# mLSTM heads: the gates' exponent rows reach 128 partitions by a transfer from memory instead of by a selection product

## The chip, the core and the metric

The kernel runs on one core of one Trainium2 chip. The metric is the device time of one execution in microseconds (us), median of several runs; less is better. A core has TensorE (PE; its weight loads are shown apart as PEld), VectorE (DVE), ScalarE (ACT), GpSimd (POOL) and SyncE (SP). Each takes its instructions in the order in which they were queued; they meet at semaphores. Transfers between memory (HBM) and the core's SBUF are issued from a queue of SP, ACT or POOL and run on 16 DMA engines. Products land in PSUM, which has eight banks of 128 x 512 f32.

## The reference

A two-layer encoder over 512 tokens of width 1024. Layer A mixes with a four-head mLSTM (head width 192) and a memory attention, layer B with a band attention and a memory attention; both are followed by a gated MLP with a causal convolution. Only the mLSTM of layer A is touched. Its core, as the reference writes it for chunks of tokens:

```python
b = jnp.cumsum(lf, axis=-1)
d = b[..., :, None] - b[..., None, :] + ii[..., None, :]
d = jnp.where(tril, d, -jnp.inf)
m_inter = b + m_st[..., None]
m_t = jnp.maximum(m_inter, jnp.max(d, axis=-1))
s = jnp.einsum('bhtd,bhsd->bhts', qq, kk) * jnp.exp(d - m_t[..., None])
num = jnp.einsum('bhts,bhse->bhte', s, vv) + ...
```

The exponent of the weight between key s and query t of a head is a sum of a term of the key and a term of the query. With the keys on the partitions, the key's term is a column (one number per partition) and the query's term is a row along the free dimension that is the same on all 128 partitions.

## The kernel before, in words

Everything is kept transposed: channels or keys on the partitions, the 512 tokens (S) along the free dimension, in four blocks (TT) of 128 (P). f32 products are made of three products of a high and a low part (`mm3`, lines L175 to L177 of the profile), so each weight tile is loaded by SP (`wr`, three buffers), cast to its high part by ACT (`wh`, L136) and subtracted to its low part by DVE (`wl`, L137).

The order of the work is woven. A generator does a stage and yields; `weave(job, filler, each)` advances a filler generator by `each` steps per yield of the job, so that TensorE has projections to do while a head's chain runs over ACT, DVE and POOL. Below that a scheduler orders each engine's queue when the program is built: an instruction that is ready may be put ahead of others, except those passed to `pin`, which stay behind everything written before them on their engine. Tiles come from pools by tag with a fixed number of buffers: 57 `u`, 8 `t`, 2 `pt`, 2 `bias` in SBUF and 3 `mm`, 3 `sc`, 2 `tr` banks in PSUM (`pmm`, `psc`, `ptr` in the profile).

The part that matters here:

- At the start two tiles `sel` (L115 memset, L118 casts) are made, with ones in the row that belongs to a head, and `maskf`, `ident` and others.
- `gate_rows` (L1026) turns the gates into rows. It is woven into the second half of the value projection and the first query and key tiles at 0.3 step per yield. Scans on DVE (L1055, L1062) give the running sums `br` and maxima `mr` of four heads on four partitions. Then, for each key block s, the query term from token 128 s on is written to `rr` (L1074, L1083). L1085 and L1086 finish the floor of the denominator. L1091 and L1092 split each row into a high part and a low part 32 partitions further down, in two zeroed `u` tiles `rp` (L1050). Eight tiny transposes (from L1096 on) make columns of `ar` and `mr`: `acol` (L1098), the key term, and the floor (L1099, an Exp on ACT).
- `mlstm_head` (L1144) runs once per head. `weighted_scores(s)` handles key block s with the n = 512 - 128 s queries from there on. It takes an `sc` bank, spreads head h's row over all partitions with one product (L1155, `sel` times `rp`, which also adds the high and the low part), and ACT takes Exp of it with the bias `acol` into a `t` tile (L1157). POOL zeroes the upper triangle of the diagonal block (L1159). After a yield come the scores in a second `sc` bank (three products and two, L175 to L177 and L525), DVE multiplies scores and weights (L1168), and ACT and DVE split the result into `pt` (L136, L137). `products(s)` multiplies these with the values into two `tr` banks. The order is scores 0, 1, 2, products 0, scores 3, products 1, 2, 3; then squares (L1195), the norm (L1202 to L1209, L237, L250) and the gate (L1216).
- Beside the heads the fillers run: `qk_tile` (accumulator L1108 in a `t` tile, taps L1111, Silu L1112), `o_tile` (L1126), query projections for the memory attention, whose zero halves POOL sets (L505), memory attention (Exp L582), then parts of the output projection.
- Later, POOL also issues the transfers of layer B's bias: a row of the table to 128 rows in memory (L1258), a corner (L1260), and from there to a `bias` tile (L1327). The final norm's gain comes by two transfers of one row of 512 to 128 partitions (L1409), also into `bias` tiles.

Of the kernel before, what the change touches and what calls it, by code (L numbers as in the profile page):

```python
# [9 lines left out]
F32 = mybir.dt.float32  # L10
F32R = mybir.dt.float32r
I32 = mybir.dt.int32
AF = mybir.ActivationFunctionType
ALU = mybir.AluOpType
AX = mybir.AxisListType

P = 128
D = 1024
S = 512
KT = D // P  # L20
TT = S // P
MEM = 256
AW = 768
AH = 4
# [26 lines left out]
def f(ap):  # L51
    return ap.bitcast(F32)
# [3 lines left out]
def trunk(  # L56
# [18 lines left out]
    nc = tc.nc  # L75
    V, A, G = nc.vector, nc.scalar, nc.gpsimd

    cpool = ctx.enter_context(tc.tile_pool(name="cpool", bufs=1))
    pool = ctx.enter_context(tc.tile_pool(name="pool", bufs=1))
    psum = ctx.enter_context(tc.tile_pool(name="psum", bufs=1, space=bass.MemoryType.PSUM))  # L80

    bufs = {"wr": 3, "wh": 3, "wl": 3, "u": 57, "t": 8, "pt": 2, "s": 16, "rb": 3, "bias": 2}
    pbufs = {"mm": 3, "sc": 3, "tr": 2}
    count = [0]
    dram = ctx.enter_context(tc.tile_pool(name="dram", bufs=1, space=bass.MemoryType.DRAM))

    def sb(tag, shape, dtype=F32):
        count[0] += 1
        return pool.tile(shape, dtype, tag=tag, name=f"{tag}{count[0]}", bufs=bufs[tag])

    def ps(tag):
        count[0] += 1
        return psum.tile([P, S], F32, tag=tag, name=f"p{tag}{count[0]}", bufs=pbufs[tag])

    def small(n=4):
# [3 lines left out]
    ident = cpool.tile([P, P], F32, name="ident")  # L99
# [9 lines left out]
        out=maskf, in_=maskf, pattern=[[1, P]], base=0, channel_multiplier=-1,  # L109
        compare_op=ALU.is_ge, fill=NEG,  # L110
    )

    sels = [cpool.tile([P, AH, P], F32R, name=f"sel{i}") for i in range(2)]
    for i, sel in enumerate(sels):
        G.memset(f(sel), 0.0)  # L115
        for s in (2 * i, 2 * i + 1):
            q = slice(32 * s, 32 * s + AH)
            V.tensor_copy(sel[q], ident[q, 32 * s : 32 * s + AH].unsqueeze(2).to_broadcast([AH, AH, P]))  # L118
    eps = cpool.tile([P, 1], F32, name="eps")
    V.memset(eps, EPS)  # L120

# [11 lines left out]
    pin = tc.keep_in_program_order  # L133
# [32 lines left out]
    def weights(*args):  # L166
        return parts(load(*args))
# [5 lines left out]
    def mm3(o, lh, ll, rh, rl, first, last, more=False):  # L173

        nc.tensor.matmul(o, lh, rh, start=first, stop=False, skip_group_check=more)  # L175
        nc.tensor.matmul(o, lh, rl, start=False, stop=False, skip_group_check=more)  # L176
        nc.tensor.matmul(o, ll, rh, start=False, stop=last, skip_group_check=more)  # L177
# [250 lines left out]
    with tc.manual_schedule(engines={mybir.EngineType.PE, mybir.EngineType.Activation, mybir.EngineType.DVE}):  # L428
# [9 lines left out]
        for q in range(KT // 2 + 1):  # L438
            if q < KT // 2:
# [6 lines left out]
                hi, lo = sb("u", [P, S], F32R), sb("u", [P, S], F32R)  # L446
# [571 lines left out]
    e, u, c, r = (cpool.tile([P, TT, AH], F32, name=f"gate{i}") for i in range(4))  # L1018
    tot = cpool.tile([AH, 16], F32, name="tot")
    acol = cpool.tile([P, TT, AH], F32, name="acol")  # L1020
    floor2 = cpool.tile([P, TT, AH], F32, name="floor2")
    RO = [0, 512, 896, 1152, 1280]

    rp = []

    def gate_rows():  # L1026

        V.tensor_copy(ic, gt[:, :, :AH])
        V.scalar_tensor_tensor(e, fg, -1.0, fg, op0=ALU.mult, op1=ALU.min)
        A.activation(e, e, AF.Exp)  # L1030
        V.tensor_scalar(u, e, 1.0, None, op0=ALU.add)
        A.activation(lf, u, AF.Ln)
        V.scalar_tensor_tensor(c, u, -1.0, e, op0=ALU.add, op1=ALU.subtract)
        V.reciprocal(r, u)
        yield
        pin(V.tensor_mul(c, c, r))
        V.tensor_tensor(out=lf, in0=lf, in1=c, op=ALU.subtract)
        V.scalar_tensor_tensor(lf, fg, 0.0, lf, op0=ALU.min, op1=ALU.subtract)
        yield
        yield  # L1040
        lfp, icp = ps("tr"), ps("tr")
        for T in range(TT):
            nc.tensor.transpose(lfp[:AH, T * P : (T + 1) * P], lf[:, T, :], ident)
            nc.tensor.transpose(icp[:AH, T * P : (T + 1) * P], ic[:, T, :], ident)
        yield
        lfr, br, ar, mr = (sb("t", [P, S])[:AH, :] for _ in range(4))
        rr = [sb("t", [P, S]) for _ in range(2)]
        rp.extend(sb("u", [P, S], F32R) for _ in range(2))
        for t in rp:
            G.memset(f(t), 0.0)  # L1050
        pin(V.tensor_copy(lfr, lfp[:AH, :]))
        yield
        for T in range(TT):
            sl = slice(T * P, (T + 1) * P)
            pin(V.tensor_tensor_scan(br[:, sl], ones[:AH, :], lfr[:, sl], 0.0, ALU.mult, ALU.add))  # L1055
        yield
        pin(V.tensor_tensor(out=ar, in0=icp[:AH, :], in1=br, op=ALU.subtract))
        yield
        carry = 0.0
        for T in range(TT):  # L1060
            sl = slice(T * P, (T + 1) * P)
            pin(V.tensor_tensor_scan(mr[:, sl], ar[:, sl], ar[:, sl], carry, ALU.max, ALU.max))  # L1062
            if T < TT - 1:
                e_ = (T + 1) * P - 1
                V.tensor_tensor(out=tot[:, T : T + 1], in0=mr[:, e_ : e_ + 1], in1=br[:, e_ : e_ + 1], op=ALU.add)
                carry = tot[:, T : T + 1]
            yield
        for s in range(TT):
            off = None
            for T in range(s, TT):  # L1070
                sl = slice(T * P, (T + 1) * P)
                dst = rr[s // 2][64 * (s % 2) : 64 * (s % 2) + AH, sl]
                if T == s:
                    pin(V.tensor_scalar(dst, mr[:, sl], -1.0, None, op0=ALU.mult))  # L1074
                else:
                    end = br[:, T * P - 1 : T * P]
                    if off is None:
                        off = end
                    else:
                        k = 4 + 4 * s + T - s  # L1080
                        V.tensor_tensor(out=tot[:, k : k + 1], in0=off, in1=end, op=ALU.add)
                        off = tot[:, k : k + 1]
                    V.tensor_scalar(dst, mr[:, sl], -1.0, off, op0=ALU.mult, op1=ALU.add)  # L1083
            yield
        pin(V.tensor_tensor(out=mr, in0=mr, in1=br, op=ALU.add))  # L1085
        V.tensor_scalar(mr, mr, -40.0, None, op0=ALU.max)  # L1086
        yield
        for s in range(TT):
            q, t = 64 * (s % 2), rp[s // 2]
            src, hi = rr[s // 2][q : q + AH, s * P :], t[q : q + AH, s * P :]  # L1090
            pin(V.tensor_copy(hi, src))  # L1091
            V.tensor_tensor(out=t[q + 32 : q + 32 + AH, s * P :], in0=src, in1=f(hi), op=ALU.subtract)  # L1092
            yield
        tp = ps("tr")
        for T in range(TT):
            nc.tensor.transpose(tp[:, T * AH : (T + 1) * AH], ar[:, T * P : (T + 1) * P], ident[:AH, :AH])  # L1096
            nc.tensor.transpose(tp[:, 16 + T * AH : 16 + (T + 1) * AH], mr[:, T * P : (T + 1) * P], ident[:AH, :AH])
        pin(V.tensor_copy(acol, tp[:, :16].rearrange("p (t h) -> p t h", t=TT)))  # L1098
        A.activation(floor2, tp[:, 16:32].rearrange("p (t h) -> p t h", t=TT), AF.Exp, scale=-2.0)  # L1099
# [44 lines left out]
    def mlstm_head(h):  # L1144
# [4 lines left out]
        pt = sb("pt", [P, 5 * S], F32R)  # L1149

        def weighted_scores(s):
            n = S - s * P
            sl = slice(s * P, (s + 1) * P)
            r = ps("sc")
            nc.tensor.matmul(r[:, :n], sels[s % 2][:, h, :], rp[s // 2][:, s * P :], start=True, stop=True)  # L1155
            e = sb("t", [P, S])
            A.activation(e[:, :n], r[:, :n], AF.Exp, bias=acol[:, s, h : h + 1])  # L1157

            G.affine_select(  # L1159
                out=e[:, :P], in_=e[:, :P], pattern=[[1, P]], base=0, channel_multiplier=-1,  # L1160
                compare_op=ALU.is_ge, fill=0.0,
            )
            yield
            o = ps("sc")
            kf, qf = ks[full], qs[full]
            mm3(o[:, :n], kf[0][:, sl], kf[1][:, sl], qf[0][:, s * P :], qf[1][:, s * P :], True, False)
            head_scores(o[:, :n], odd, qs[sh], slice(s * P, S), ks[sh], sl, False, True)
            V.scalar_tensor_tensor(e[:, :n], o[:, :n], DH**-0.5, e[:, :n], op0=ALU.mult, op1=ALU.mult)  # L1168
            split(pt[:, RO[s] : RO[s + 1]], pt[:, 1280 + RO[s] : 1280 + RO[s + 1]], e[:, :n])
            yield  # L1170
# [3 lines left out]
        def products(s):  # L1174
            if not nums:
                nums.extend(ps("tr") for _ in range(2))
            for o, c in zip(nums, (3 * P, 2 * P) if odd else (0, P)):
                mm3(
                    o[:, s * P :], vh[hp][s][:, c : c + P], vl[hp][s][:, c : c + P],
                    pt[:, RO[s] : RO[s + 1]], pt[:, 1280 + RO[s] : 1280 + RO[s + 1]], s == 0, s == TT - 1,  # L1180
                )
# [88 lines left out]
    for j in range(KT):  # L1270
        wh, wl = weights(rows(ffn_w_down[0], j * P, P, FT - LAST, FT), LAST, P)
# [175 lines left out]
    n = LAST // 2  # L1447
    for hf in range(2):
# [6 lines left out]
        for Ts, pieces in groups:  # L1455
            for c in pieces:
                if c.start:
                    os_[Ts[0]] = ps("mm")
                for u in range(n):
# [3 lines left out]
                    wh, wl = ws[u]  # L1463
# [61 lines left out]
```

## Time and profile before

| | us |
|---|---|
| median of 3 runs | 1197.71 (1197.57 to 1198.04) |
| span of the profiled execution | 1197.4 |
| PE busy | 1186.5 |
| DVE busy | 967.3 |
| ACT busy | 718.4 |
| POOL busy | 123.3 |
| first and last selection product (L1155) | start at 105.3 and 238.0 |

How to read the rows that follow. A row of the order of time has start, duration, engine, line, operation, output tile, input tiles, shape, count, and in brackets how long the engine had been idle and what it waited for. A row of groups has the count behind the x, then busy time and mean ns of one, then idle time before them with what ended most of it. A row of waits says who waited for whom, the total in us, how often, and the longest. A row of one line has the durations of one in ns as min/median/max and the first and the last start. A row of transfers has the issuing queue, the count, the KB of each and the median us from issue to landing. Buffer numbers are left out of tile names.

### The profile page before, as it was taken

What the parts mean: (1) busy time and instruction counts of PE and PEld (TensorE: products, weight loads), DVE (VectorE), ACT (ScalarE), POOL (GpSimd) and SP (SyncE); (2) the same over time, 40 slices, a digit from 0 to 9 for tenths busy, and PEclk for the clock granted to TensorE, in tenths of its full rate; (3) what the DMA queues carried; (4) which work ended last, traced back from release to release, by engine and by line L of the source; (5) the groups of instructions that cost most, each with busy time, mean ns of one, the idle gap of its engine ahead of it and who ended that gap; (6) DMA issues with size and microseconds to landing.
All of it is one profiled execution on the core that took longest, in us unless ns stands there. A gap on an engine that the chain in (4) does not pass through costs nothing.

```text
span 1197.4 us, 18206 instructions
## 1 busy us (share of the span) xinstructions
PE 1186.5 (99%) x6735; PEld 1039.1 (87%) x6735; DVE 967.3 (81%) x1772; ACT 718.4 (60%) x1290; POOL 123.3 (10%) x206
## 2 busy tenths in 40 slices
PE   9999999999999999999999999999999999999997
PEld 8988888888889989999888888888889988999986
DVE  6778688878978888888698888997897888888855
ACT  5646577655655555555575667776565655555545
POOL 1200101000021111111021000001001011011100
PEclk9999999999999999999999999999999999999999
DMA  8634111454266666665563223146336466665551
GB/s 283 212 92 123 54 54 57 134 152 133 88 157 162 153 162 155 151 144 129 152 189 120 89 71 99 55 130 201 116 89 150 110 138 141 141 141 136 121 158 71
DMA packets 199131, 155.97 MB, mean 130 GB/s; under 512 B 7976, under 2 KB 179458, under 8 KB 199042
## 3 DMA queue, kind: packets, MB, share of 16 engines
q1 hardware_dynamic: 183906, 119.74, 34.2%
q0 software_dynamic: 14560, 34.02, 13.7%
q8 instruction: 53, 0.87, 0.3%
q10 hardware_dynamic: 576, 1.05, 0.2%
q14 instruction: 36, 0.29, 0.1%
HBM read 126.27 MB, written 32.44 MB: 133 GB/s over the span
## 4 chain that ended last, share of the span: by engine, by line
PE 93%; DMA 2%; ACT 2%; DVE 2%; issue 0%; SPq 0%; ACTq 0%; DVEq 0%
PE pmm L175 15%; PE pmm L176 15%; PE pmm L177 15%; PE ptr L175 6%; PE ptr L177 6%; PE ptr L176 6%; PE pmm L791 6%; PE psc L177 5%; PE psc L175 5%; PE psc L176 5%; PE pmm L790 3%; PE psc L525 2%; DMA wr<-in_mem_w_kv_dram 2%; PE ptr L1352 1%; PE ptr L1373 1%; PE ptr L1374 1%
## 5 line engine op out<-in xcount | busy, mean ns | idle before, releaser
L175 PE MATMUL pmm<-u,wh 128*128 128x512 f32 (+1 forms) x872 | 309.1, 355 | 0.3 <-ACT u L136 0.2
L176 PE MATMUL pmm<-u,wh 128*128 128x512 f32 (+1 forms) x872 | 306.3, 351 | 0.0
L177 PE MATMUL pmm<-u,wl 128*128 128x512 f32 (+1 forms) x872 | 306.3, 352 | 0.0
L137 DVE TENSOR_TENSOR wl<-wr,wh 128x1024 fp32r<-128x1024 f32 (+3 forms) x172 | 199.8, 1163 | 55.1 <-ACT wh L136 53.1
L136 ACT CAST wh<-wr 128x1024 fp32r<-128x1024 f32 (+3 forms) x172 | 172.1, 1002 | 99.8 <-PE pmm L176 45.2
L177 PEld LDWEIGHTS pmm<-u,wl 128*128 128x128 f32 x872 | 164.5, 189 | 20.9
L175 PEld LDWEIGHTS pmm<-u,wh 128*128 128x128 f32 x872 | 164.5, 189 | 18.7 <-ACT u L136 1.1
L176 PEld LDWEIGHTS pmm<-u,wh 128*128 128x128 f32 x872 | 164.7, 189 | 18.3 <-DVE u L137 0.5
L175 PE MATMUL ptr<-u,wh 128*128 128x512 f32 x272 | 106.7, 392 | 0.0
L177 PE MATMUL ptr<-u,wl 128*128 128x512 f32 x272 | 106.1, 390 | 0.0
L176 PE MATMUL ptr<-u,wh 128*128 128x512 f32 x272 | 105.9, 389 | 0.0
L759 POOL DMA_DIRECT2D xspill<-t x64 | 55.5, 867 | 462.5 <-ACT t L758 457.1
L136 ACT CAST u<-pt 128x512 fp32r<-128x512 f32 x102 | 62.8, 618 | 47.2 <-DVE pt L881 47.1
L137 DVE TENSOR_TENSOR u<-pt,u 128x512 fp32r<-128x512 f32 x102 | 69.9, 689 | 11.2 <-ACT u L136 8.5
L175 PE MATMUL psc<-u,wh 128*128 128x256 f32 (+1 forms) x232 | 76.1, 328 | 0.0
L177 PE MATMUL psc<-u,wl 128*128 128x256 f32 (+1 forms) x232 | 75.9, 327 | 0.0
L176 PE MATMUL psc<-u,wh 128*128 128x256 f32 (+1 forms) x232 | 75.9, 327 | 0.0
L791 PE MATMUL pmm<-u,u 128*128 128x512 f32 x192 | 69.6, 397 | 0.0
L943 ACT ACTIVATE t<-t 128x512 f32<-128x512 f32 x34 | 21.5, 632 | 79.4 <-DVE t L666 79.4
L827 DVE TENSOR_TENSOR t<-t,pmm 128x256 f32<-128x256 f32 x72 | 30.2, 420 | 45.0 <-ACT t L825 45.0
L758 ACT COPY t<-ptr 128x512 f32<-128x512 f32 x64 | 37.4, 584 | 42.8 <-PE ptr L177 42.8
L666 DVE SCALAR_TENSOR_TENSOR t<-t,cols,t 128x511 f32<-128x511 f32 x80 | 59.6, 746 | 3.7 <-ACT t L673 3.7
(305 smaller groups left out, 2671.5 us busy)
## 6 DMA issues: line engine op xcount, KB each, us to landing
wr<-in_ffn_w_up_dram SPq DMA_DIRECT2D x54, 512.0 KB, 4.5
wr<-in_ffn_w_down_dram SPq DMA_DIRECT2D x38, 512.0 KB, 4.1
pt<-in_ffn_w_up_dram SPq DMA_DIRECT2D x34, 512.0 KB, 6.0
xspill<-t POOLq DMA_DIRECT2D x64, 256.0 KB, 5.2
wr<-in_a_w_in_dram SPq DMA_DIRECT2D x20, 512.0 KB, 3.7
xspill<-u POOLq DMA_DIRECT2D x32, 256.0 KB, 2.7
u<-xspill SPq DMA_DIRECT2D x32, 256.0 KB, 5.1
wr<-in_w_kv_dram SPq DMA_DIRECT2D x12, 512.0 KB, 3.8
```

The source lines that it names most:

```text
L136: high = A.copy(hi, src) if on_act else V.tensor_copy(hi, src)
L137: low = V.tensor_tensor(out=lo, in0=src, in1=f(hi), op=ALU.subtract)
L175: nc.tensor.matmul(o, lh, rh, start=first, stop=False, skip_group_check=more)
L176: nc.tensor.matmul(o, lh, rl, start=False, stop=False, skip_group_check=more)
L177: nc.tensor.matmul(o, ll, rh, start=False, stop=last, skip_group_check=more)
L525: nc.tensor.matmul(o, a, b, start=first and i == 0, stop=i == 1)
L666: V.scalar_tensor_tensor(acc[:, n:], src[:, : S - n], self.fw[:, c * FT + j : c * FT + j + 1], acc[:, n:], op0=ALU.mult, op1=ALU.add,)
L758: A.copy(t, o)
L759: G.dma_start(xspill[j], t, accum_op=ALU.add)
L790: nc.tensor.matmul(r[:, :H], w[1][:, k], p[i - 1][:, :H], start=False, stop=False, skip_group_check=True)
L791: nc.tensor.matmul(r, w[0][:, k], p[i - 1], start=False, stop=k == n - 1, skip_group_check=True)
L827: V.tensor_tensor(out=o, in0=o, in1=r[:, H:], op=ALU.add)
```

## The change

The rows are not spread by TensorE any more. After the row of block s is in `rr`, POOL issues a write of it, in f32, to a tile `exponents` in memory. When the four writes are issued, POOL issues the first four spreads (head 0, blocks 0 to 3), each a transfer that reads one row 128 times into a `bias` tile. In `weighted_scores` Exp reads that tile, and right behind it POOL issues the spread of the step four further on, that is of the same block of the next head, ahead of the masking. The selection tiles, the split of the rows with its four yields, and the two zeroed `u` tiles go. The tag `bias` has four buffers instead of two, also for layer B and the final norm.

```diff
-    bufs = {"wr": 3, "wh": 3, "wl": 3, "u": 57, "t": 8, "pt": 2, "s": 16, "rb": 3, "bias": 2}
+    bufs = {"wr": 3, "wh": 3, "wl": 3, "u": 57, "t": 8, "pt": 2, "s": 16, "rb": 3, "bias": 4}
...
-    sels = [cpool.tile([P, AH, P], F32R, name=f"sel{i}") for i in range(2)]
-    for i, sel in enumerate(sels):
-        G.memset(f(sel), 0.0)
-        for s in (2 * i, 2 * i + 1):
-            q = slice(32 * s, 32 * s + AH)
-            V.tensor_copy(sel[q], ident[q, 32 * s : 32 * s + AH].unsqueeze(2).to_broadcast([AH, AH, P]))
...
+    NEXT = 4
     RO = [0, 512, 896, 1152, 1280]
 
-    rp = []
+    exponents = dram.tile([TT, AH, S], F32, name="exponents")
+    order = [(h, s) for h in range(AH) for s in range(TT)]
+    spreads = {}
+
+    def spread_exponents(i):
+        if i < len(order):
+            h, s = order[i]
+            row = exponents[s, h : h + 1, s * P :]
+            spreads[h, s] = sb("bias", [P, S])[:, : S - s * P]
+            src = bass.AP(tensor=row.tensor, offset=row.offset, ap=[[0, P], [1, S - s * P]])
+            pin(G.dma_start(spreads[h, s], src))
...
         rr = [sb("t", [P, S]) for _ in range(2)]
-        rp.extend(sb("u", [P, S], F32R) for _ in range(2))
-        for t in rp:
-            G.memset(f(t), 0.0)
...
                     V.tensor_scalar(dst, mr[:, sl], -1.0, off, op0=ALU.mult, op1=ALU.add)
+            q = 64 * (s % 2)
+            pin(G.dma_start(exponents[s, :, s * P :], rr[s // 2][q : q + AH, s * P :]))
             yield
+        for i in range(NEXT):
+            spread_exponents(i)
...
-        for s in range(TT):
-            q, t = 64 * (s % 2), rp[s // 2]
-            src, hi = rr[s // 2][q : q + AH, s * P :], t[q : q + AH, s * P :]
-            pin(V.tensor_copy(hi, src))
-            V.tensor_tensor(out=t[q + 32 : q + 32 + AH, s * P :], in0=src, in1=f(hi), op=ALU.subtract)
-            yield
...
-            r = ps("sc")
-            nc.tensor.matmul(r[:, :n], sels[s % 2][:, h, :], rp[s // 2][:, s * P :], start=True, stop=True)
             e = sb("t", [P, S])
-            A.activation(e[:, :n], r[:, :n], AF.Exp, bias=acol[:, s, h : h + 1])
-
+            A.activation(e[:, :n], spreads.pop((h, s)), AF.Exp, bias=acol[:, s, h : h + 1])
+            spread_exponents(order.index((h, s)) + NEXT)
```

## The prediction

> **What bounds the kernel now.** I read the page's head and engine shares first, then the stretch in which the mLSTM heads run as one window, then what TensorE waited for, then its order of time around the product that is removed.
>
> ```profile
> span 1197.4 us, 18206 instructions
> PE 1186.5 (99%) x6735; PEld 1039.1 (87%) x6735; DVE 967.3 (81%) x1772; ACT 718.4 (60%) x1290; POOL 123.3 (10%) x206
> 80.00:245.00 165.00, 164.80 (x838) 138.65 (x836) 129.32 (x256) 109.61 (x189) 10.74 (x22) 1.00 0.30 87
> PE psc L175 <- ACT t L1157: 0.2, 1, 0.2
> PE pmm L175 <- ACT u L136: 0.2, 1, 0.2
> ```
>
> The third line is the window from 80 to 245 us: busy time of PE, PEld, DVE, ACT and POOL, then granted clock, DMA share and GB/s. PE is busy for 164.80 of 165.00 us at full clock, DVE for 78% and ACT for 66%, and all PE waits from 100 to 300 us are the two lines of 0.2 us. So in this stretch a matmul that disappears should shorten the kernel by the slot it held, and a delay elsewhere costs only what is longer than PE's reserve of queued work. That slot is not its listed duration, because matmuls overlap: it is the distance to the next start.
>
> ```profile
> 105.26 0.40 PE L1155 MATMUL psc<-u,sel 128*128 128x512 f32 x1
> 105.50 0.39 PE L175 MATMUL pmm<-u,wh 128*128 128x512 f32 x1
> 105.73 0.40 PE L176 MATMUL pmm<-u,wh 128*128 128x512 f32 x1
> ...
> 108.00 0.34 PE L1155 MATMUL psc<-u,sel 128*128 128x384 f32 x1
> 108.18 0.40 PE L175 MATMUL pmm<-u,wh 128*128 128x512 f32 x1
> ...
> 111.17 0.28 PE L1155 MATMUL psc<-u,sel 128*128 128x256 f32 x1
> 111.29 0.40 PE L175 MATMUL pmm<-u,wh 128*128 128x512 f32 x1
> ...
> 116.00 0.22 PE L1155 MATMUL psc<-u,sel 128*128 128x128 f32 x1
> 116.06 0.45 PE L175 MATMUL pmm<-u,wh 128*128 128x512 f32 x1
> 116.35 0.40 PE L176 MATMUL pmm<-u,wh 128*128 128x512 f32 x1
> ```
>
> **Part 1, the products.** Per head the four selection products hold 0.24, 0.18, 0.12 and 0.06 us. The product behind the last one takes 0.29 us to the next start where its like takes 0.23 (105.50 to 105.73), so the short one costs 0.12. That is 0.66 us a head and 2.6 us for four. Lower bound: 0.23 us per 512 columns, so 1280 columns give 0.57 us a head, 2.3 us in all. Upper bound: the 5.0 us that the line is listed as busy; it counts time in which the next product runs too, so no more than 0.3 of the way to it belongs in the range. I take 2.6, since the starts measure it directly.
>
> Each product also held a score bank until Exp had read it, and here PE met that once:
>
> ```profile
> L1155 PE MATMUL psc<-u,sel 128*128 128x512 f32 (+3 forms) x16 | 5.0, 311 | 0.0
> 235.61 0.44 PE L175 MATMUL psc<-u,u 128*128 128x384 f32 x1 [0.18 <-ACT t L1157]
> ```
>
> With half the demand on the three score banks that 0.2 us should go too. Sum on PE: -2.8 us.
>
> **Part 2, VectorE, the start and the buffers.** The high and low parts of the rows (L1091, L1092) leave DVE, and so do the selection casts at the start.
>
> ```profile
> L1092 DVE TENSOR_TENSOR u<-t,u 4x512 fp32r<-4x512 f32 (+3 forms) x4 | 1.9, 483 | 0.1
> L1091 DVE CAST u<-t 4x512 fp32r<-4x512 f32 (+3 forms) x4 | 1.2, 312 | 0.1
> L118 DVE CAST sel<-ident x4: 417/420/704, 2.2 to 3.8; 4x512 fp32r<-4x512 f32 x4
> ```
>
> That is 3.1 us around 84 to 94 us and about 2 us (four times 0.42 to 0.70) before 4.2 us. DVE is not the bound in either place, and PE's start waits for the first transfers, so I count 0 for both (between 0 and -0.4 us, the size of the waits above). Two `u` buffers become free and `rr` can be released when its writes have landed, which can only loosen. The steps of the gate rows that follow move four steps earlier in a weave of 0.3 step per yield, about 13 yields. They issue eight tiny transposes, one DVE copy and one ACT Exp, all before PE needs them: 0. Four `bias` tiles instead of two let the band attention's transfers start earlier, and nothing in the profile waits for those: 0.
>
> **Part 3, the row's way to 128 partitions.** Added are 4 writes of at most 8 KB and 16 transfers of 256, 192, 128 and 64 KB per head, all issued on POOL. Nearest rows: `rep<-maskf` for the small writes to memory, and `bias<-in_final_g`, which copies one row to 128 partitions just as here.
>
> ```profile
> rep<-maskf POOLq DMA_DIRECT2D x12, 16.0 KB, 3.5
> bias<-in_final_g_dram POOLq DMA_DIRECT2D x2, 256.0 KB, 4.7
> L1409 POOL DMA_DIRECT2D bias<-in_final_g_dram x2: 683/716/748, 807.5 to 808.9; - x2
> 82.25 0.22 DVE L1074 TENSOR_SCALAR t<-t 4x128 f32<-4x128 f32 x1
> 109.38 0.72 POOL L1159 TENSOR_SCALAR_AFFINE_SELECT t<-t 128x128 f32<-128x128 f32 x2 [66.00 <-ACT t L1157]
> 108.57 1.15 ACT L1157 ACTIVATE t<-psc,acol 128x512 f32<-128x512 f32 x2
> 136.06 0.69 ACT L1157 ACTIVATE t<-psc,acol 128x512 f32<-128x512 f32 x1 [1.92 <-PE psc L1155]
> 190.23 0.69 ACT L1157 ACTIVATE t<-psc,acol 128x512 f32<-128x512 f32 x1
> 234.87 1.16 ACT L1157 ACTIVATE t<-psc,acol 128x512 f32<-128x512 f32 x2
> ```
>
> The last row is computed at 82.5 us (the instruction at 82.25 takes 0.22). Write issued by 83.2, landed by 86.7; four spreads issued behind it by 89.6, the last landed by about 94.3. The first Exp ran at 108.57, so 14 us cover this. POOL stands at the waits for the row writes meanwhile, but it had nothing to do for 66 us. Later, a spread is issued when the Exp four steps back has freed its buffer, and its own Exp comes one head later: 27, 54 and 45 us by the three distances above, against under 6 us of issue and landing. Cost: 0. It is 4.7 us once per head with no cover, 19 us at most.
>
> POOL does gain a queue: at 12 of the 16 steps the masking of the diagonal block (L1159) stands behind a transfer's issue of 0.7 us, and DVE's multiplication (L1168) and the casts to `pt` wait for it. The reserve there is the smallest I found:
>
> ```profile
> 111.66 1.16 DVE L137 TENSOR_TENSOR pt<-t,pt 128x512 fp32r<-128x512 f32 x2 [0.22 <-ACT pt L136]
> 113.96 0.39 PE L175 MATMUL ptr<-pt,u 128*128 128x512 f32 x1
> ```
>
> The parts are done at 112.82 and used at 113.96: 1.1 us. Against the 0.7 us stands that Exp no longer waits for a product (4.2 us over four times, next line) and can run any time before the scores exist, so that the masking may be through by then. I count 0, and 12 times 0.7, 8.6 us, were the reserve gone at every step.
>
> ```profile
> L1157 ACT ACTIVATE t<-psc,acol 128x512 f32<-128x512 f32 (+3 forms) x16 | 8.2, 525 | 4.3 <-PE psc L1155 4.2
> ```
>
> The Trainium skill speaks against this part: SBUF — State Buffer, section "SBUF: two separate sides", says that transfers issued from GpSimd cannot have their descriptors written while VectorE holds the port pair that the two share, and gives about 3.1 us for an issue that takes 0.62 us alone. The issues in this trace don't show it: 0.68 to 0.75 us above, and the twelve `bias` issues of the band attention stay at 0.55 to 0.75 with DVE busy for 164 of 190 us. But POOL work does stretch here:
>
> ```profile
> L1159 POOL TENSOR_SCALAR_AFFINE_SELECT t<-t x16: 287/299/1254, 109.4 to 238.7; 128x128 f32<-128x128 f32 x16
> L1327 POOL DMA_DIRECT2D bias<-rep x12: 546/548/748, 627.5 to 782.7; - x12
> 620.00:810.00 190.00, 189.35 (x971) 157.22 (x970) 164.47 (x401) 131.96 (x299) 18.34 (x32) 1.00 0.33 99
> ```
>
> A masking of 0.30 us has taken 1.25 at worst, so such a block is worth 1 us a time. That is a rival below.
>
> **The sum.** The profiled execution spans 1197.4 us, 0.3 under the median of 1197.71. 1197.4 - 2.6 - 0.2 = 1194.6, and with the 0.3 that lies around it **1194.9 us**.
>
> **The rivals.**
>
> (B) *Part is given back.* ACT takes its queue in order. Where an Exp is placed ahead of its transfer's landing, or between two Silus so that it brings a pair of table loads, what stands behind it is late:
>
> ```profile
> L1112 ACT ACT_TABLE_LOAD x6 | 7.7, 1283 | 9.8 <-DVE t L1111 6.5 <-DVE s L1209 3.3
> ACT wh L136 <- PE pmm L176: 8.7, 9, 1.8
> ```
>
> A pair is 2.6 us of ACT. Weight casts run as soon as PE frees the buffer (second line), and with three buffers that is two projections ahead, each 24 products of 0.23 us, 5.4 us; that hides a pair. The `pt` reserve of 1.1 us does not, so each such event costs up to 1.5 us. One or two events: 1194.9 + 1.5 to + 3, about 1197.
>
> (C) *Slower: Exps that run ahead hold the `t` tiles.* Until now Exp could not start before its product. Now only a landed row and a free `t` tile hold it back, so the next heads' Exps may run early, and each keeps one of eight `t` tiles until its scores exist.
>
> ```profile
> 114.89 0.77 ACT L1108 ACTIVATE t<-pmm,cols 128x512 f32<-128x512 f32 x1
> 123.11 1.09 ACT L1195 ACTIVATE t<-ptr 128x512 f32<-128x512 f32 x2 [1.91 <-PE ptr L177]
> 125.01 0.79 ACT L1108 ACTIVATE t<-pmm,cols 128x512 f32<-128x512 f32 x1
> 137.73 0.67 DVE L1168 SCALAR_TENSOR_TENSOR t<-psc,t 128x512 f32<-128x512 f32 x1
> ```
>
> Between heads 0 and 1 the kernel needs two tiles for squares and one or two for the convolution's accumulators. With four Exps held it still fits; from six on the accumulator at 125.01 has no tile until the next head's first multiplication at 137.73, 12.7 us later. Three `pmm` banks give PE two projections, 10.9 us, so the stall is 1.8 us if only one is late, and up to 12.7 if the work that frees the tile queues behind it. The middle, about 7, at one of the heads gives 1201.5; at all three 1216. For it: ACT is idle for a third of the window and POOL's memsets for later tiles already run tens of us ahead. Against it: a transfer's buffer comes free only one step at a time.
>
> (D) *The port holds POOL up.* 20 issues and 16 maskings, each stretched by 1 us, of which those at 12 steps meet the reserve of 1.1 us. If two in three pass it by 1 us, PE loses 8 us: 1203. By the skill's 3.1 us for an issue it would be 2.4 us later per step, 1.3 beyond the reserve, an estimate of 12 times 1.3, 16 us.
>
> (E) *No gain.* The products filled slots that PE spends waiting for the next operands anyway: 1197.7. PE's 0.2 us of waits speaks against it.
>
> **How the numbers follow.** A (forecast) 0.47, B 0.18, C 0.27, D 0.05, E 0.03. About 0.2%, 2.4 us, is what a measurement of this kernel can tell from no change: faster is below 1195.3, slower above 1200.1. A's own range is 1194.0 (2.6 + 0.3 x 2.4 of the products, with the 0.2 and the 0.3 of the sum) to 1195.8; most of it, 0.38, lies below 1195.3 and 0.09 above. B and E are within (0.21); of C 0.02 is within and 0.25 above, and D is above. So faster 0.38, same 0.32, slower 0.30. The range goes up to 1203, so that C at one head is in; C at several heads and half of D, about 0.14, are out, and below 1194.0 I leave 0.04.
>
> **What would show it.** Right: no L1155, PE's busy time in the heads' stretch shorter by 2 to 3 us with waits still under 1 us; the first Exp not waiting for a transfer; POOL's new issues at 0.5 to 0.9 us. B: ACT waits on DMA `bias`, or more table loads than six before 245 us under L1112. C: Exps far ahead of their L1168, L1108 late, PE waiting for `pmm`. D: issues or maskings above 1 us, and L1168 waiting for L1159 much more than now. Wrong altogether would be a PE stall in a stage that the diff does not touch, which would mean that the order of the whole program has moved.

## The result and the profile after

The changed kernel takes 1194.92 us (median of 9 runs, 1194.77 to 1195.72), the kernel before 1197.71 (9 runs beside it, 1197.57 to 1198.71). The ratio is 0.9975, with a 95% interval of 0.9967 to 0.9983: about 2.8 us faster.

The page's head and engine shares of the changed kernel:

```profile
span 1194.0 us, 18184 instructions
PE 1183.5 (99%) x6719; PEld 1037.0 (87%) x6719; DVE 961.7 (81%) x1760; ACT 725.2 (61%) x1294; POOL 130.3 (11%) x222
```

PE has 16 matmuls fewer and is busy for 3.0 us less; DVE lost 5.6 us and ACT and POOL each gained about 7. To see where the time went, one stretch is enough. It begins with the last spill of the memory attention's keys and values ahead of the heads (the last start of line L377 before, L371 after) and ends with the first spill behind them (the first start of L640, then L634). Rows of those lines, before and then after; behind the durations stand the first and the last start:

```profile
L377 POOL DMA_DIRECT2D memkv<-u x4: 539/551/741, 15.5 to 38.3; - x4
L640 POOL DMA_DIRECT2D xspill<-u x16: 539/539/557, 259.6 to 841.4; - x16
```

```profile
L371 POOL DMA_DIRECT2D memkv<-u x4: 542/554/736, 14.9 to 37.8; - x4
L634 POOL DMA_DIRECT2D xspill<-u x16: 542/542/564, 256.5 to 838.0; - x16
```

From 38.3 to 259.6 is 221.3, from 37.8 to 256.5 is 218.7: the stretch is 2.6 us shorter (the unrounded starts give 221.2 and 218.7). It is the measure for most of what follows, since the start of the kernel differs from one execution to the next: over all profiles here the last of those four spills starts between 36.8 and 38.3 us, except in the run with maskings of a constant tile, where those fill POOL's start and it comes at 41.6. The same stretch as a window, columns as before (busy time of PE, PEld, DVE, ACT, POOL with counts, clock, DMA share, GB/s), for the kernel before and for the one after, and for the latter also the window that the prediction read:

```profile
38.30:259.60 221.30, 220.94 (x1136) 190.16 (x1135) 169.96 (x348) 132.98 (x223) 15.69 (x44) 1.00 0.33 97
```

```profile
37.80:256.50 218.70, 218.22 (x1120) 187.87 (x1119) 166.58 (x340) 137.99 (x227) 23.94 (x62) 1.00 0.41 110
80.00:245.00 165.00, 164.68 (x839) 138.73 (x838) 127.91 (x254) 115.10 (x193) 20.37 (x43) 1.00 0.40 103
```

1136 matmuls became 1120, PE's idle time in it went from 0.36 to 0.48 us, and the stretch shrank with the matmuls. PE's waits from 100 to 300 us after the change are again two of 0.2 us. The first, at 252.3, was there before (at 255.4); the second, at 233.5, stands where before the wait for a score bank was, at 235.6:

```profile
PE pmm L169 <- ACT u L130: 0.2, 1, 0.2
PE ptr L169 <- ACT pt L130: 0.2, 1, 0.2
```

The new work of the changed kernel in the views of one line: the spreads' issues with their landing, the writes' issues with theirs, and the masking.

```profile
L1029 POOL DMA_DIRECT2D bias<-exponents x16: 547/566/572, 83.0 to 193.7; - x16
...
DMA to landing us min/median/max: 3.2/3.9/7.7
```

```profile
L1087 POOL DMA_DIRECT2D exponents<-t x4: 499/514/552, 75.1 to 82.5; - x4
...
DMA to landing us min/median/max: 1.5/1.6/2.8
```

```profile
L1157 POOL TENSOR_SCALAR_AFFINE_SELECT t<-t x16: 285/307/702, 101.1 to 234.7; 128x128 f32<-128x128 f32 x16
```

From the order of time, the four spreads of head 0:

```profile
82.96 2.21 POOL L1029 DMA_DIRECT2D bias<-exponents x4
```

The last spread of head 0 is issued by 85.2 and landed by 92.9 at the slowest. ACT's table loads and Exps (L1155) of the changed kernel in order of time, then three of its groups:

```profile
98.21 1.28 ACT L1155 ACT_TABLE_LOAD   x1
99.50 0.73 ACT L1155 ACTIVATE t<-bias,acol 128x512 f32<-128x512 f32 x1
100.25 1.28 ACT L1112 ACT_TABLE_LOAD   x1
104.92 1.28 ACT L1155 ACT_TABLE_LOAD   x1
106.22 0.62 ACT L1155 ACTIVATE t<-bias,acol 128x384 f32<-128x384 f32 x1
...
118.01 1.28 ACT L1112 ACT_TABLE_LOAD   x1 [2.83 <-DVE t L1111]
131.54 1.28 ACT L1155 ACT_TABLE_LOAD   x1
132.84 0.73 ACT L1155 ACTIVATE t<-bias,acol 128x512 f32<-128x512 f32 x1
```

```profile
L1112 ACT ACT_TABLE_LOAD x8 | 10.3, 1283 | 13.6 <-DVE t L1111 10.3 <-DVE s L1207 3.3
L1155 ACT ACTIVATE t<-bias,acol 128x512 f32<-128x512 f32 (+3 forms) x16 | 8.8, 561 | 0.1
L1155 ACT ACT_TABLE_LOAD x4 | 5.1, 1283 | 0.1
```

No Exp waits for a transfer (0.1 us idle before all 16). The first runs at 99.50 instead of 108.57, between two Silus (L1112), and so brings its own table loads: eight and four where the kernel before has six and two. The four more are 5.1 us of ACT; no wait of PE stands behind them.

### The profile page after: what moved, and what is told of

It reads as the page before. It is cut to its first block, busy times and chain, and to the rows that moved or that the text cites. A ratio compares the mean times of both kernels' runs of the same rounds, so it can differ in the third digit from the quotient of the medians.

```text
span 1194.0 us, 18184 instructions
## 1 busy us (share of the span) xinstructions
PE 1183.5 (99%) x6719; PEld 1037.0 (87%) x6719; DVE 961.7 (81%) x1760; ACT 725.2 (61%) x1294; POOL 130.3 (11%) x222
## 4 chain that ended last, share of the span: by engine, by line
PE 92%; ACT 3%; DVE 2%; DMA 1%; SPq 1%; issue 0%; POOL 0%; POOLq 0%; DVEq 0%; ACTq 0%
PE pmm L169 15%; PE pmm L170 15%; PE pmm L171 15%; PE ptr L171 6%; PE ptr L169 6%; PE ptr L170 6%; PE pmm L785 6%; PE psc L171 5%; PE psc L170 5%; PE psc L169 5%; PE pmm L784 3%; PE psc L519 2%; PE ptr L1350 1%; DMA wr<-in_mem_w_kv_dram 1%; PE ptr L1371 1%; PE ptr L1372 1%
```

## The experiments

Each is an edit of the changed kernel unless it says otherwise. "Stretch" is the one above, 218.7 after and 221.2 before. The kernel before has medians from 1197.71 to 1198.16 us in different sessions, so the ratio to the kernel before, measured beside each, is what is compared; the changed kernel has 0.9975.

**The changed kernel again**, as a control in a later session:

> The changed kernel once more, as the control for the two kernels beside it on this chip: 0.9975 of the kernel before, within 0.001.

1195.11 us, ratio 0.9975 (0.9964 to 0.9986), stretch 218.6. The ratio repeats; the median is 2.65 us below that of the kernel before, measured beside it.

**Are the slots the gain? The products put back.** One product per step into a score bank that nobody reads:

```diff
+            r = ps("sc")
+            nc.tensor.matmul(r[:, :n], onesr, act[0][0][:, s * P :], start=True, stop=True)
             e = sb("t", [P, S])
```

> The changed kernel with one product put back per step (same shape, of a constant and an activation tile, into a score bank that nobody reads). PE-slot theory: only the slots come back, 16 of them worth 2.6 us, so 1197.5 (1197.1 to 1198.0), about the kernel before less 0.2 to 0.5. Rival, that the gain came from what else left (selection tiles at the start, split rows on VectorE, score banks held until Exp): stays at 1194.9 to 1195.5.

1198.53 us, ratio 1.0003 (0.9994 to 1.0011): all of the gain is given back and 1 us more than was expected; the stretch is 222.3, longer by 3.6. Their start distances are those of the selection products, 0.23, 0.18, 0.12 and 0.06 us with the same 0.06 on the product behind the last, so 2.6 of the 3.6 are slots. Most of the rest is one stall, in the order of time:

```profile
120.87 0.39 PE L170 MATMUL pmm<-u,wh 128*128 128x512 f32 x1
121.10 0.39 PE L171 MATMUL pmm<-u,wl 128*128 128x512 f32 x1
122.03 0.33 PE L169 MATMUL ptr<-pt,u 128*128 128x128 f32 x1 [0.54 <-ACT pt L130]
122.36 0.33 PE L170 MATMUL ptr<-pt,u 128*128 128x128 f32 x1
```

From 121.10 to 122.03 are 0.93 us where 0.23 are due, and the product behind takes 0.33 to the next start where it takes 0.06: 1.0 us. The wait is listed with 0.54, because the listed duration of the matmul ahead (0.39) covers part of the gap. A stall of PE is read from the distance of starts; the idle time shows half of it here. In the changed kernel PE does not wait there. The trace shows where `pt` becomes late: ACT stands at the landing of a weight tile before it casts it.

```profile
115.26 1.05 ACT L130 CAST wh<-wr 128x1024 fp32r<-128x1024 f32 x1 [2.05 <-DMA wr<-in_a_w_in_dram]
```

In the changed kernel this cast starts at 114.12 without a wait for a transfer. VectorE's work behind it is late too, and the cast to `pt` starts at 121.70 against 119.84, with PE at the same product in both at 117.5. Why that tile landed later was not tried.

**The products alone taken from the kernel before.** Exp reads a constant tile instead of a bank, so the query's term of the exponent is left out; everything else, the split of the rows and the selection tiles too, stays:

```diff
-            r = ps("sc")
-            nc.tensor.matmul(r[:, :n], sels[s % 2][:, h, :], rp[s // 2][:, s * P :], start=True, stop=True)
...
-            A.activation(e[:, :n], r[:, :n], AF.Exp, bias=acol[:, s, h : h + 1])
+            A.activation(
+                e[:, :n].rearrange("p (a b) -> p a b", b=P), ones.unsqueeze(1).to_broadcast([P, n // P, P]),
+                AF.Exp, bias=acol[:, s, h : h + 1],
+            )
```

> The kernel before with the sixteen selection products and their score banks taken out and nothing else: Exp reads a constant instead (the gates' query term is left out of the output), the selection tiles and the split of the rows stay and go unused. If the products' slots are the whole gain, the same time as the changed kernel beside it, within 0.4 us. If the selection tiles, the split rows or the two tiles of the pool have a part in it, up to 0.5 us slower than that.

1194.96 us, ratio 0.9976 (0.9966 to 0.9985). The window of the stretch:

```profile
36.80:255.50 218.70, 218.26 (x1120) 187.89 (x1119) 169.55 (x348) 132.89 (x223) 14.32 (x44) 1.00 0.33 98
```

The same 218.7 with DVE's 348 instructions still there: the whole gain in the stretch is the products, and the 3 us that DVE lost are worth nothing. This run also has the table loads of the kernel before, six and two, so the four that the changed kernel adds cost it nothing.

**Do the transfers cost anything? None at all.** No write and no spread; Exp reads a tile of zeros (the query's term is left out again). The tag `bias` has three buffers here:

```diff
+    flat = cpool.tile([P, S], F32, name="flat")
+    V.memset(flat, 0.0)
...
-            spreads[h, s] = sb("bias", [P, S])[:, : S - s * P]
...
-            pin(G.dma_start(spreads[h, s], src))
+            spreads[h, s] = flat[:, : S - s * P]
...
-            pin(G.dma_start(exponents[s, :, s * P :], rr[s // 2][q : q + AH, s * P :]))
```

> The changed kernel without any of the 20 transfers: Exp reads a constant row tile (the gates' query term is left out of the output). If the transfers, POOL's issues and their traffic cost nothing, as the prediction counted: 1194.9 within 0.4. If they give back part of a larger gain: 1193.5 or less.

1195.28 us, ratio 0.9978 (0.9969 to 0.9987), stretch 218.7. Twenty issues and the 2.6 MB of 16 spreads fewer change nothing: the new work is wholly beside PE's.

**The selection tiles built again at the start** (into `bias` tiles, read by nobody):

```diff
+    sels = [sb("bias", [P, S], F32R).rearrange("p (a b) -> p a b", a=AH) for i in range(2)]
+    for i, sel in enumerate(sels):
+        G.memset(f(sel), 0.0)
...
```

> The changed kernel with the two selection tiles still made at the start (two memsets on POOL, four casts on VectorE), never read. If the start of the kernel got shorter because these left, as the profiles' 0.5 us by the first spill on POOL suggest, 1195.4; if they were hidden behind the first transfers as the prediction counted, 1194.9 within 0.3.

1195.11 us, ratio 0.9974 (0.9963 to 0.9984). Hidden, as counted.

**How far ahead must a spread be issued?** One step instead of four, and two with two buffers:

```diff
-    NEXT = 4
+    NEXT = 1
```

> The changed kernel with NEXT = 1: a row is fetched only when the Exp of the step before has run, instead of four steps ahead. A landing took 2.9 to 7.7 us, steps inside a head are about 3 us apart. If it is the cover of a whole head that makes the transfers free, the later Exps of each head wait for theirs and with them VectorE's multiplication: 1197 to 1203, with ACT waits on bias. If PE's queued work hides even that: 1194.9 to 1195.6.

1197.22 us, ratio 0.9992 (0.9984 to 1.0001), stretch 220.4. Now the landing shows as a wait of ACT (who waited for whom, total, times, longest):

```profile
ACT t L1155 <- DMA bias<-exponents: 4.7, 4, 2.0
```

Only four of 16 Exps meet it, and of the 4.7 us PE sees 1.7.

```diff
-    bufs = {... "rb": 3, "bias": 4}
+    bufs = {... "rb": 3, "bias": 2}
...
-    NEXT = 4
+    NEXT = 2
```

> The changed kernel with NEXT = 2 and two bias buffers instead of four, for layer B too. Two steps ahead is about 6 us inside a head against 3.6 us median to landing, so the heads lose little: 1195.0 to 1196.0. From the first layer-B bias row on, the profiles before and after differ by 0.3 us; if the two more buffers there made it, that stretch goes back to its old length, if not it stays 0.3 us shorter.

1196.18 us, ratio 0.998 (0.9971 to 0.9989), stretch 219.7: 1 us of the 2.6 is lost, and the time is just above the range that was expected. By the ratio alone this run can't be told from the changed kernel (the intervals overlap; with one step ahead they don't); the stretch tells them apart.

**Do Exps that run early cost or save?** The Exps kept in written order on ACT:

```diff
-            A.activation(e[:, :n], spreads.pop((h, s)), AF.Exp, bias=acol[:, s, h : h + 1])
+            pin(A.activation(e[:, :n], spreads.pop((h, s)), AF.Exp, bias=acol[:, s, h : h + 1]))
```

> The changed kernel with the sixteen Exps kept in the written order on ACT, so that they can't run ahead between the Silus of head 0. ACT then loads two table sets fewer, 2.6 us of its time. If ACT's extra loads are hidden: 1194.9 within 0.3. If they gave part of the gain back (rival B): down to 1193.5.

1198.93 us, ratio 1.0008 (1.0 to 1.0017), stretch 221.9. Both expectations missed: with two table loads fewer it is 3.2 us slower. Its window and the clearest of its stalls, in the order of time:

```profile
37.40:259.30 221.90, 220.38 (x1120) 187.33 (x1119) 166.97 (x340) 135.38 (x225) 23.36 (x62) 1.00 0.41 108
```

```profile
235.54 0.45 PE L169 MATMUL pmm<-u,wh 128*128 128x512 f32 x1
236.46 0.74 PE L169 MATMUL ptr<-pt,u 128*128 128x512 f32 x2 [0.47 <-ACT pt L130]
```

The matmuls are the same 1120, PE's idle time rose by 1.0 us only, and its busy time by 2.2: part of that is again stalls that the listed durations cover (0.92 us between these two starts, with 0.47 listed). A late Exp makes masking, multiplication and `pt` late. DVE now waits for the masked tile at eight steps, 6.0 us in all, where in the changed kernel it waits at five, 1.3 us:

```profile
DVE t L1166 <- POOL t L1157: 6.0, 8, 1.7
```

So Exps that run early are worth more than the table loads that they bring.

**How much later may the masking be?** First, four maskings of a constant tile ahead of each, which is pinned behind them:

```diff
+            for _ in range(4):
+                pin(G.affine_select(
+                    out=maskf, in_=maskf, pattern=[[1, P]], base=0, channel_multiplier=-1,
+                    compare_op=ALU.is_ge, fill=NEG,
+                ))
```

> The changed kernel with four more maskings of a constant tile (0.28 us each, 1.1 us) on POOL between each step's transfer issue and its masking. If the masking is through well before VectorE needs it: 1194.9 within 0.4. If the reserve is the 1.1 us that the prediction read between the parts and their first use, and the issue has taken 0.6 of it: about 0.6 us at each of 12 steps, 1200 or more.

1195.65 us, ratio 0.998 (0.997 to 0.999). It says nothing on the question: the extra maskings depend on no Exp and were placed at the start, where POOL is busy for 25 of the first 30 us. So the masking itself was done five times on the same tile, which makes it about 1.1 us later at each step:

```diff
-            G.affine_select(
+            for _ in range(5):
+                G.affine_select(
...
```

> The changed kernel with the masking done five times on the weight tile itself (each time the same result), so that every step's masking ends four times 0.28, about 1.1 us, later than now. If Exp runs early enough for the masking to be done before the scores exist: 1194.9 within 0.5. If the reserve is 1.1 us less the 0.6 us of the issue, it is overdrawn by 0.6 us at most steps: 1198 or more.

1203.01 us, ratio 1.0044 (1.0031 to 1.0056), stretch 226.6: 7.9 us longer. Waits of DVE and of PE, and windows around the last of the stalls:

```profile
DVE t L1167 <- POOL t L1158: 10.0, 11, 1.4
...
PE ptr L170 <- DVE pt L131: 3.0, 3, 1.1
PE ptr L169 <- ACT pt L130: 1.3, 3, 0.8
```

```profile
236.00:240.60 4.60, 3.07 (x14) 1.87 (x12) 2.85 (x6) 3.52 (x7) 4.39 (x15) 1.00 0.83 228
240.60:244.00 3.40, 3.29 (x9) 2.74 (x10) 2.46 (x7) 0.70 (x2) 1.10 (x4) 0.50 0.01 2
```

DVE waits at 11 steps, and part of that reaches PE. Behind the stalls of 236 to 240.6, 1.53 us in all, the granted clock is 0.50 for 3.4 us, which is 1.7 of the 7.9. So the reserve holds a masking behind one issue of 0.57 us, and does not hold 1.1 more.

**A version beyond: the head norm's row by a transfer too.** Two products with a diagonal per head, of 512 columns each, spread the norm's factor over the partitions (L250 before, L244 here). For heads 0 to 2 the factors are written to memory, 512 pieces of 4 bytes, and read back with one transfer to 128 partitions:

```diff
-        dg = diagonal(fc)
-        yield 2.673
-        fb = spread(dg, "sc")
+        if h < 3:
+            G.dma_start(bass.AP(tensor=factors[h].tensor, offset=factors[h].offset, ap=[[1, P], [P, TT]]), fc)
+            fb = sb("rb", [P, S])
+            G.dma_start(fb, bass.AP(tensor=factors[h].tensor, offset=factors[h].offset, ap=[[0, P], [1, S]]))
+            yield 2.673
...
```

> The changed kernel with the same step taken for the head norm of heads 0 to 2: the factor goes to memory (512 pieces of 4 bytes) and one transfer copies the row to 128 partitions, in place of two products of 512 columns and two diagonal tiles per head. By slots, 6 products of 0.23 us: 1.4 us less than the changed kernel, 1193.5. Rival: POOL stands at the wait for the write, some 4 us, and the next head's masking or transfers behind it are late: no gain, or up to 4 us slower per head.

1223.8 us, ratio 1.0212 (1.0198 to 1.0226). Waits of DVE, POOL and PE:

```profile
DVE u L1221 <- DMA rb<-factors: 28.5, 3, 12.4
...
POOL rb L1213 <- DMA factors<-s: 25.2, 3, 8.7
...
PE psc L519 <- ACT u L503: 11.2, 1, 11.2
PE ptr L588 <- DVE t L579: 7.1, 2, 5.4
```

The stretch is 247.1, which is 28.4 us longer, over 9 us a head and more than either expectation. Unlike the exponents, this row is used at once: DVE stands in its queue for up to 12.4 us of a round trip, and the work of the next head stands behind it. Part of the loss is the clock: in three pieces of the stretch, 27.3 us in all, it is 0.51 to 0.52, with PE busy for 15.3 of them, so some 8 us at most. For heads 0 and 1 alone, with the multiplication that needs the row put off until the next head's products are written (and the products kept for the others):

```diff
+        while late:
+            late.pop()()
...
+        def gated():
+            for j, r in ((full, slice(0, P)), (sh, rs)):
+                pin(V.tensor_tensor(out=og[j][r, :], in0=fb[r, :], in1=og[j][r, :], op=ALU.mult))
...
+        if h < 2:
+            late.append(gated)
+        else:
+            gated()
```

> The same idea as in the run before (the head norm's row by a write and a transfer instead of four products with a diagonal), for heads 0 and 1 only, and with the gating multiplications that read it put off until the last products of the next head are written, pinned there on VectorE. If the 28 us of the run before came only from VectorE standing at the round trip, what is left are the slots: 2 heads of the four N=128..512 products' columns, about 0.23 us per 512 columns and at least 0.45 to 0.9 us in all, so 1194.2 +- 0.4 (ratio 0.9967 to 0.9972) and a heads' stretch of 217.8 to 218.2. The rival: POOL stands at the landing of the factors' write (8 us then), and the maskings and spreads of the next head queue behind it; with the reserve behind a masking between 0.6 and 1.7 us that would cost PE 5 us or more per head, 1200 to 1212, with DVE waiting for POOL's masked tile and PE for pt.

1205.09 us, ratio 1.0063 (1.005 to 1.0077), stretch 228.9. The rival's time came, but not by its way, and the saving at stake was smaller than written above: two products a head, 0.9 us for two heads. Rows of the order of time (POOL, DVE, PE), then three windows:

```profile
130.32 0.79 POOL L1215 DMA_DIRECT2D factors<-s  x1 [2.81 <-DVE s L222]
140.49 0.54 POOL L1217 DMA_DIRECT2D rb<-factors  x1 [8.81 <-DMA factors<-s]
...
146.17 0.69 DVE L1227 TENSOR_TENSOR u<-rb,u 128x512 f32<-128x512 f32 x1 [3.10 <-DMA rb<-factors]
...
147.15 0.39 PE L171 MATMUL pmm<-u,wl 128*128 128x512 f32 x1
150.16 0.38 PE L1205 MATMUL psc<-mcf,t 128*128 128x2 f32 x2 [2.63 <-ACT t L1198]
...
259.81 1.31 PE L169 MATMUL pmm<-u,wh 128*128 128x512 f32 x3 [1.87 <-ACT u L130]
```

```profile
148.00:150.00 2.00, 0.00 (x0) 0.00 (x0) 1.31 (x3) 1.11 (x2) 0.00 (x0) 1.00 0.42 35
150.00:158.00 8.00, 7.74 (x27) 6.69 (x28) 5.34 (x11) 2.42 (x5) 0.00 (x0) 0.57 0.25 68
260.40:263.80 3.40, 3.40 (x10) 2.60 (x9) 0.69 (x1) 0.00 (x0) 0.00 (x0) 0.52 0.52 154
```

POOL stands at the write's landing and issues the read 10.2 us after the write, and DVE meets the landing at 146.17, 15.9 us after the write was issued, though the multiplication had been put off by a head. No masking stood behind POOL (those of that head had run by 127.5). ACT's casts wait for DVE, the squares (L1198) for ACT, PE for the squares: 2.6 us without work, and then 8 us at a clock of 0.57, which is 3.4 us more. PE also waits 1.9 us near the end of the stretch, with 3.4 us at a clock of 0.52 behind it, which is 1.6 more, and 0.8 us at two places between. Together these are 10.3 us of the 11.1 to be explained (10.2 that the stretch is longer, and 0.9 of slots saved). No version beat the changed kernel.

## Why the prediction was right, point by point

**The slots (2.6 us).** Shown from both sides: the products alone taken from the kernel before shorten the stretch from 221.2 to 218.7, and put back they hold the same start distances. The lower bound (2.3) leaves out the 0.06 us on the product behind the 128-column one; the upper one (5.0, the listed durations) is nearly twice what was gained. The lower end of the forecast's own range, from its terms 2.6, 0.3 x 2.4, 0.2 and 0.3, comes out at 1194.2 and not 1194.0; nothing hangs on it.

**The wait for the score bank (0.2 us).** This term failed in its net: the wait is gone, but at nearly the same place PE now waits 0.2 us for `pt`. The stretch gained 2.6, not 2.8. That the medians still differ by 2.79 us may come from the band attention: between the last spill in its first half (625.8 before, 622.7 after) and the last one behind it (841.4 and 838.0) lie 215.6 and 215.3 us. Over all profiles here this distance is 215.4 to 215.6 us with two `bias` tiles (three profiles), 215.4 with three (one), and 215.2 to 215.3 with four, but for one of 215.5 (the last run of the experiments). So the four tiles, which the prediction put at 0, are perhaps worth 0.2 us; that one exception leaves it open. That the forecast meets the median to 0.02 us is luck: 0.2 us of its sum did not come in the way it named.

**The sum's 0.3 us around the span.** The reading was wrong and cancelled out. The profiled execution of the changed kernel took 1195.72 us with a span of 1194.0: 1.7 us lie around a span. If as much lies around the 1197.4 of before, that execution was about 1.4 us above the median; that of after is 0.8 above. Since the forecast only took a difference from it, nothing came of it.

**DVE, the start and the buffers (0).** Right: selection tiles built again cost nothing, and the split of the rows left in place costs nothing.

**The transfers (0).** Right, and by the route given: the estimate for head 0's last landing was 94.3, the rows give 92.9 at the slowest, and the first Exp comes at 99.50. The slowest landing, 7.7 us, is longer than the "under 6 us of issue and landing" of the prediction; the cover of a head was far more. Without any transfer the stretch is the same. Issued one step ahead they cost 1.7 us, so the distance of a head is what hides them.

**The masking behind an issue (0).** Right, and thin: a masking behind an issue of 0.57 us cost nothing, 1.1 us more at each step cost 7.9. The reserve that the prediction read from one place, 1.1 us, was of the right order.

**B, table loads.** They came: four more, with Exps between two Silus. They cost nothing, not 1.5 us each: the run with the products alone taken out has four loads fewer, the run without transfers has them all, and both have the same stretch of 218.7. The first Exp runs 7.3 us ahead of its multiplication (99.50 against 106.80); that this is why, is argued and not tried.

**C, Exps that hold `t` tiles.** Did not come. Before the next heads' first Exps (132.84, 188.31, 230.53) their spreads had long landed, yet they run 4.4, 2.3 and 1.2 us ahead of the multiplications, not a head. That early Exps help is shown by the pinned run; what kept them from running further ahead was not tried.

**D, the port.** Did not come: all 16 issues take 547 to 572 ns with DVE busy for 127.9 of the window's 165 us, and the longest masking takes 702 ns, where before one took 1254. The Trainium skill's rule for this (SBUF — State Buffer, "SBUF: two separate sides"), some 3.1 us for a starved issue, is not seen in this trace. The price that the prediction set on such a delay, 8 us, is near what the fivefold masking measured, 7.9, but 1.7 of that are the lower clock, which the prediction's sum did not have.

**E, no gain.** Refuted by the products put back.

## What to carry to other kernels

Where TensorE has no idle time, a matmul that is removed is worth the distance of starts that it held, not its listed duration, and a stall is likewise read from the distance of starts. A row can be moved from a product to a transfer for nothing if it exists a stage before it is used: here the last landing of the first head was over by 92.9 us and the first use came at 99.50, while a row that is used at once cost 28 us for three heads, whose six products hold 1.4. What rides behind the new issues on their queue has its own reserve; make that work later on purpose to learn how much is left.

## What the runs showed of the hardware that was not expected

- A write of 2 KB in 512 pieces of 4 bytes is slow to land. The two views of the line that issues it, with three heads and then with two, against 1.5 to 2.8 us for the rows of the exponents:

```profile
DMA to landing us min/median/max: 8.6/8.9/9.2
```

```profile
DMA to landing us min/median/max: 8.2/9.1/9.9
```

- Short stalls bring the clock down. In the last run a gap of 2.6 us was followed by 8 us at 0.57, and one of 1.9 us by 3.4 us at 0.52; with the fivefold masking, 1.5 us of idle time within 4.6 was followed by 3.4 us at 0.50. Each cost about its own length again. The Trainium skill (TensorE: Matmul & The Clock Gate, "Part 1: The HAM clock gate") puts the return to half clock behind an idle window of about 3.4 us; the half clock agrees, but the second and the third came after less idle time than that, and so did the first, unless the products of two columns that run from its end to 150.89 count as idle.
- Four added table loads (4 x 1.283 us) cost nothing where ACT was busy for 70% of the time, and late Exps cost more than the two loads that they saved.
